# Right operands of the first feed-forward product, formed product by product, with their transposes between the early products

## The chip, the cores and the metric

One Trainium2 chip, one of its cores. The metric is the time of one execution on the device in microseconds, as the median of three runs. The engines are TensorE (PE, with its weight loads PEld), VectorE (DVE), ScalarE (ACT), GpSimd (POOL) and SyncE (SP, which issues the DMAs).

## The reference

A decoder block in float32: sequence 1024, model width 1024, one layer. Two branches (an RWKV-7 mix and a sparse attention) are merged by gates and projected back; then comes the feed-forward part with a hidden width of 4096, and a last norm. What matters here is its last third:

```python
x = x + merged @ w_out[l]
h2 = rms_norm(x, g_ffn[l])
x = x + jnp.square(jax.nn.relu(h2 @ w_ffn_up[l])) @ w_ffn_down[l]
return rms_norm(x, g_final)
```

## The kernel before

**Number format.** Each float32 operand of a large product is split into a high half (a copy to fp32r by ACT) and a low half (source minus high half, by DVE or POOL); `part` does that. A product is then three matmuls per block of 128 channels: high by high, high by low, low by high (`mm3`, lines 242 to 244). `mm3y` issues the same three through `pe`, which also ties each matmul to the one `window[0]` places earlier in the written order (a tie for the planner that adds no wait on the chip); `tr` does so for a transpose.

**Order of work.** The kernel is written as a sequence. A planner puts each instruction in its engine's queue when, by its own simulated costs, its inputs and a free room are there; earlier written instructions have precedence. Rooms of a tag (`bufs`) go round: a new tile waits until an old one is given back. The ties of `pe` bound how far TensorE's order may leave the written one.

**Gates and output projection** (lines 1328 to 1430). For eight blocks d of channels the gates are loaded into `gp`, a room of the tag `g8` (6 rooms of 128 x 2048 floats; d = 0 has one of its own), then tanh, products and sums give `merged[d]` (lines 1176 to 1186). The first loads of `x1` are tied behind the load of d = 7. Then `merged @ w_out` runs, c = 0 to 3, and its results are added to x (line 1430).

**Norm.** `normed(half)` forms the normalised rows `xs` of 512 tokens in two `g8` rooms (lines 1353 to 1357). `norm_first`, inside the output projection, transposes the first half of the tokens, keeps it as `raw0[0..7]` in two `g8` rooms ("hr") and forms the right operands R2 and R4.

**First feed-forward product.** h2 @ w_up is computed by Strassen's scheme with seven products of half size. For each of 16 blocks f of 128 + 128 hidden columns there are products 2, 4, 1, 5, 7, 3, 6, each of 4 x 3 matmuls of 128x512 with a right operand R[p] (the activations, made once for all f) and a left operand (weights, made per f). With B11 = raw0[0..3], B21 = raw0[4..7] and the second half of the tokens as B12 (pa) and B22 (pb), R2 = B11, R4 = B21 - B11, R1 = B11 + B22, R5 = B22, R7 = B21 + B22, R3 = B12 - B22, R6 = B11 + B12. `plan` lists entries: products (2, 4) of f = 0, 1, 2 first (PRE = 3; the early products), then (1, 5), (7, 3), (6) of f = 0, 1, 2, then all four entries of f = 3 and so on. The left operands are built two entries ahead (`up_ops`, `up_operands`): a load into `st` (3 rooms), a sum on POOL into `k2` (3 rooms, line 1462), then `part` into `w` (3 rooms). `up_product` adds results from the up rooms (6 of 128x512 in PSUM) to C (a `g8` room); after product 6 five sums are formed on DVE, three of them in kc (a `g8` room), and both are stored.

**norm_second** (lines 1386 to 1411) is called when the early products have all been written (i == PRE). For each k of 0 to 3 it transposes two blocks of the second half (`channels`, two rooms `small`), forms c1, c7, c6 and b22 in `k2` rooms, three of them by VectorE's scalar_tensor_tensor (STT) and b22 by ACT and later an STT, and splits each result into R1, R5, R7, R3 and R6 of that k.

The second feed-forward product (line 1540 on) follows; it uses `g8` for x1 (4 tiles) and o (4 tiles).

```python
            c1, c7, c6 = k2("c"), k2("c"), k2("c")
            STT(c1, pb, gb, raw0[k], op0=OP.mult, op1=OP.add)
            part(R[1][k][:, 0], R[1][k][:, 1], c1, nc.gpsimd)
```

Of the kernel before, what the change touches and what calls it, by code (L numbers as in the profile page):

```python
# [9 lines left out]
F32 = mybir.dt.float32  # L10
# [13 lines left out]
P = 128  # L24
# [71 lines left out]
def hybrid_block(ctx: ExitStack, tc: tile.TileContext, a, out, dbg=None, stop=99):  # L96
# [16 lines left out]
    def small():  # L113
        return psm_[0].tile([P, 512], F32, name="sm")
# [84 lines left out]
    def pull(gen, n):  # L199
        for _ in range(n):  # L200
            if next(gen, "end") == "end":
                return
# [1112 lines left out]
    psa[0] = psf_stack.enter_context(tc.tile_pool(name="psf", bufs=3, space=PSUM))  # L1315

    def g8(name):
        return mp.tile([P, 4, 512], F32, name=name, tag="g8", bufs=6)

    def k2(name):  # L1320
        return mp.tile([P, 512], F32, name=name, tag="k2", bufs=3)

    def part(hi, lo, src, eng):
        nc.scalar.activation(hi, src, AF.Copy)  # L1324
        eng.tensor_tensor(lo, src, hi.bitcast(F32), op=OP.subtract)  # L1325
# [3 lines left out]
    for d in range(8):  # L1329
        if d == 0:  # L1330
            gg, pp = gates1[0]
        else:
            gp = g8("gp")
            gg, pp = gp[:, 0:2], gp[:, 2]
            ld = gate_load(gg, pp, d, 1)
        if d % 2 == 0:
            w = next(ws)
        ps = acc()[:, 0:512]
        for k in range(4):
            mm3(ps, [w[:, s_, k, (d % 2) * P:(d % 2 + 1) * P] for s_ in range(2)],  # L1340
                [yT1[k][:, s_, :] for s_ in range(2)], start=(k == 0), stop=(k == 3))
        gate_merge(merged[d], gg, pp, ps)
# [14 lines left out]
            nc.vector.tensor_scalar(xs[j], xt[j], r[:, j:j + 1], None, op0=OP.mult)  # L1357
        return xs

    def channels(xs, k):  # L1360
        ps = small()
        for j in range(4):
            nc.tensor.transpose(ps[:, j * P:(j + 1) * P], xs[j][:, k * P:(k + 1) * P], ident)
        return ps, pcol("gffn", k)


    R = {}
    raw0 = []

    def norm_first():  # L1370
        xs = normed(0)
        room = [g8("hr") for _ in range(2)]
        raw0.extend(room[k // 4][:, k % 4] for k in range(8))
        for p in (2, 4):
            R[p] = [hp[0].tile([P, 2, 512], F32R, name="h2", tag=f"hT0_{4 * (p == 4) + k}") for k in range(4)]
        for k in (0, 4, 1, 5, 2, 6, 3, 7):
            ps, g = channels(xs, k)
            nc.scalar.activation(raw0[k], ps, AF.Copy, scale=g)
            if k < 4:
                part(R[2][k][:, 0], R[2][k][:, 1], raw0[k], nc.vector)  # L1380
            else:
                c = k2("c")
                nc.gpsimd.tensor_tensor(c, raw0[k], raw0[k - 4], op=OP.subtract)
                part(R[4][k - 4][:, 0], R[4][k - 4][:, 1], c, nc.vector)

    def norm_second(xs):
        def h2(k, n):
            if n < 8:
                return mp.tile([P, 2, 512], F32R, name="h2", tag="mh", bufs=8)
            if n < 18:  # L1390
                return mp.tile([P, 2, 512], F32R, name="h2", tag="x4", bufs=10)
            return base.tile([P, 2, 512], F32R, name="h2", tag="ev", bufs=2)

        for i, p in enumerate((1, 5, 7, 3, 6)):
            R[p] = [h2(k, 4 * i + k) for k in range(4)]
        for k in range(4):
            pa, ga = channels(xs, k)
            pb, gb = channels(xs, k + 4)
            STT = nc.vector.scalar_tensor_tensor
            c1, c7, c6 = k2("c"), k2("c"), k2("c")  # L1400
            STT(c1, pb, gb, raw0[k], op0=OP.mult, op1=OP.add)
            part(R[1][k][:, 0], R[1][k][:, 1], c1, nc.gpsimd)
            b22 = k2("c")
            nc.scalar.activation(b22, pb, AF.Copy, scale=gb)
            part(R[5][k][:, 0], R[5][k][:, 1], b22, nc.gpsimd)
            STT(c7, pb, gb, raw0[k + 4], op0=OP.mult, op1=OP.add)
            part(R[7][k][:, 0], R[7][k][:, 1], c7, nc.vector)
            STT(b22, pa, ga, b22, op0=OP.mult, op1=OP.subtract)
            part(R[3][k][:, 0], R[3][k][:, 1], b22, nc.vector)
            STT(c6, pa, ga, raw0[k], op0=OP.mult, op1=OP.add)  # L1410
            part(R[6][k][:, 0], R[6][k][:, 1], c6, nc.gpsimd)

    for c in range(4):
        if c == N2:
# [60 lines left out]
    def up_product(f, p, l):  # L1475
        ps = psu.tile([P, 512], F32, name="up")
        for k in range(4):
            mm3(ps, [l[s_][:, k] for s_ in range(2)], [R[p][k][:, s_] for s_ in range(2)],
                start=(k == 0), stop=(k == 3))
        if p == 2:  # L1480
            CB[f] = g8("C")
        c11, c12, c21, c22 = [CB[f][:, i] for i in range(4)]
        TT = nc.vector.tensor_tensor
        if p == 2:
            nc.scalar.activation(c22, ps, AF.Copy)
        elif p == 4:
            TT(c21, ps, c22, op=OP.add)
            nc.scalar.activation(c11, ps, AF.Copy)
            hidden(c21)
        elif p == 1:  # L1490
            TT(c11, ps, c11, op=OP.add)
            TT(c22, ps, c22, op=OP.subtract)
        elif p == 5:
            TT(c11, c11, ps, op=OP.subtract)
            nc.scalar.activation(c12, ps, AF.Copy)
        elif p == 7:
            TT(c11, ps, c11, op=OP.add)
            hidden(c11)
        elif p == 3:
            TT(c12, ps, c12, op=OP.add)  # L1500
            TT(c22, ps, c22, op=OP.add)
            hidden(c12)
        else:
            TT(c22, ps, c22, op=OP.add)
            hidden(c22)
            kc = g8("kc")
            TT(kc[:, 2], c11, c21, op=OP.add)
            TT(kc[:, 0], c11, c22, op=OP.add)
            TT(kc[:, 1], c12, c22, op=OP.add)
            nc.sync.dma_start(hc_dram[f, 4:7].rearrange("s p t -> p s t"), kc[:, 0:3])  # L1510
            TT(c12, c12, c11, op=OP.subtract)
            TT(c21, c21, c22, op=OP.subtract)
            nc.sync.dma_start(hc_dram[f, 0:4].rearrange("s p t -> p s t"), CB.pop(f))
# [21 lines left out]
        return up_operands(up_blocks(f, prods), prods)  # L1535

    ops = [up_ops(0), up_ops(1)]
    for i, (f, prods) in enumerate(plan):
        if i == PRE:
            norm_second(xs1)  # L1540
        l = ops.pop(0)
        for p in prods:
            up_product(f, p, l[p])
        ops.append(up_ops(i + 2))


# [63 lines left out]
    def square(t, i):  # L1610
        cs = slice(i * 512, (i + 1) * 512)
        if t not in ssq:
            if t % 2 == 0:
                o2 = g8("o").rearrange("p a b -> p (a b)")
                rooms.extend([o2[:, 0:D], o2[:, D:2 * D]])
            ssq[t] = mp.tile([P, 4], F32, name="ss", tag=f"ssf{t}"), rooms[t]
        ss, o = ssq[t]
        nc.scalar.activation(o[:, cs], x1[t][:, cs], AF.Square, accum_out=ss[:, i:i + 1])
# [88 lines left out]
```

## Time and profile before

| what | value |
|---|---|
| median of three runs | 1836.25 us (1833.04, 1836.25, 1837.2) |
| the profiled execution: time, span | 1827.06 us, 1825.3 us |
| mean granted TensorE clock in it | 0.961 |
| TensorE busy in it | 1692.4 us, 93% of the span |
| VectorE, ScalarE, GpSimd busy | 1320.5, 896.9, 841.7 us (72, 49, 46%) |
| DMA, mean over the span | 132 GB/s |

The profile tells of one execution; times in it run from the span's start. "Busy" is the time in which an engine has an instruction in work, waiting for a port or for memory included. The granted clock is a share of full speed. Shapes such as 128x512 are partitions by elements. The first feed-forward product lies between 1167 and 1497 us, the second from there to the end.

### The profile page before, as it was taken

Reading aid. Unit: us, or ns where it says so; the run is one execution under the profiler, and the core shown is the slowest. Engines: PE = TensorE matmul, PEld = TensorE weight load, DVE = VectorE, ACT = ScalarE, POOL = GpSimd, SP = SyncE. Lnnn points to the kernel's source line nnn. Section 1 sums busy time; section 2 is a strip of 40 time slices with the busy share of each in tenths; the row PEclk is TensorE's granted clock in tenths of the full one; section 3 lists DMA queues with packets and bytes.
Section 4 is the critical chain, followed back from the end, with each engine's and each line's share of the span. In section 5 each row is a group of like instructions: output and inputs, shape, how many; then the busy total and the mean of one; then the engine's idle time right before and its main releaser. Section 6 shows DMA issues by size and latency. Waiting matters only on the chain.

```text
span 1825.3 us, 27191 instructions
## 1 busy us (share of the span) xinstructions
PE 1692.4 (93%) x9554; PEld 1419.5 (78%) x9554; DVE 1320.5 (72%) x2597; ACT 896.9 (49%) x1751; POOL 841.7 (46%) x765
## 2 busy tenths in 40 slices
PE   6999999949999999998999898879999999999996
PEld 6988887738878777777877798857888887888884
DVE  6689946996777453678676556679888885765887
ACT  5375565717777434354535334544444444444443
POOL 1523566414343343343425432367666655545554
PEclk9999999979999998999878999999999999999998
DMA  5230353212311454345345466315545358643543
GB/s 173 75 116 29 116 144 105 66 41 89 116 35 36 138 151 132 99 137 163 109 123 170 154 226 251 105 60 170 174 137 180 128 185 299 207 141 91 171 124 127
DMA packets 267247, 241.52 MB, mean 132 GB/s; under 512 B 64268, under 2 KB 205894, under 8 KB 267110
## 3 DMA queue, kind: packets, MB, share of 16 engines
q1 hardware_dynamic: 267110, 239.78, 41.9%
q8 instruction: 75, 1.23, 0.3%
q14 instruction: 62, 0.51, 0.1%
HBM read 164.24 MB, written 75.50 MB: 131 GB/s over the span
## 4 chain that ended last, share of the span: by engine, by line
PE 60%; DVE 21%; DMA 8%; ACT 4%; issue 4%; POOL 2%; SPq 1%; DVEq 0%; ACTq 0%; POOLq 0%
PE dn L189 14%; PE up L243 8%; PE up L244 8%; PE up L242 8%; PE sm L189 5%; DVE jk L577 3%; DVE w L1325 2%; PE sm L192 2%; PE acc L189 2%; PE dn L243 2%; PE dn L244 2%; PE ch L189 2%; PE dn L242 2%; DMA zt<-zd 1%; DVE Zt L998 1%
## 5 line engine op out<-in xcount | busy, mean ns | idle before, releaser
L189 PE MATMUL dn<-hT,w 128*128 128x512 f32 (+1 forms) x1488 | 377.7, 401 | 8.3 <-ACT last L673 7.6
L189 PEld LDWEIGHTS dn<-hT,w 128*128 128x128 f32 (+1 forms) x1488 | 272.9, 188 | 67.1 <-ACT last L673 10.1
L1325 DVE TENSOR_TENSOR w<-st,w 128x512 fp32r<-128x512 f32 x224 | 236.6, 1089 | 78.7 <-ACT w L1324 78.3
L210 POOL TENSOR_TENSOR w<-st,w 128x1024 fp32r<-128x1024 f32 (+2 forms) x75 | 179.3, 2391 | 162.9 <-ACT w L209 143.7
L1324 ACT ACTIVATE w<-st 128x512 fp32r<-128x512 f32 x224 | 132.5, 624 | 168.2 <-PE up L244 50.8
L242 PE MATMUL up<-h,w 128*128 128x512 f32 x448 | 177.5, 397 | 7.4 <-ACT h L1324 5.9
L243 PE MATMUL up<-h,w 128*128 128x512 f32 x448 | 176.3, 394 | 2.2 <-DVE h L1325 1.4
L244 PE MATMUL up<-h,w 128*128 128x512 f32 x448 | 175.6, 393 | 1.6 <-DVE w L1325 1.6
L1588 POOL TENSOR_TENSOR st<-wb,wb 128x512 f32<-128x512 f32 x80 | 119.5, 1498 | 91.2 <-DVE w L1325 59.4
L243 PE MATMUL up<-w 128*128 128x512 f32 x384 | 150.2, 393 | 5.1 <-DVE ss L1606 3.3
L244 PE MATMUL up<-w 128*128 128x512 f32 x384 | 149.6, 392 | 0.0
L1462 POOL TENSOR_TENSOR c<-st 128x512 f32<-128x512 f32 x80 | 124.0, 1560 | 42.9 <-DVE w L1325 20.1
L209 ACT ACTIVATE w<-st 128x1024 fp32r<-128x1024 f32 (+2 forms) x91 | 94.7, 1041 | 42.9 <-PE acc L244 15.0
L242 PE MATMUL up<-w 128*128 128x512 f32 x384 | 108.0, 392 | 0.2
L242 PEld LDWEIGHTS up<-h,w 128*128 128x128 f32 x448 | 84.6, 189 | 28.5 <-ACT h L1324 9.2
L1473 POOL TENSOR_TENSOR C<-C 128x512 f32<-128x512 f32 x64 | 75.8, 1185 | 66.7 <-ACT C L1472 66.7
L577 DVE TENSOR_SCALAR_CACHE_REDUCE jk<-room,cand 128x384 bf16<-128x384 int16 (+2 forms) x96 | 92.7, 1009 | 15.1 <-ACT jk L590 14.1
L243 PEld LDWEIGHTS up<-h,w 128*128 128x128 f32 x448 | 85.0, 190 | 21.1 <-DVE h L1325 2.5
L244 PEld LDWEIGHTS up<-h,w 128*128 128x128 f32 x448 | 84.8, 189 | 21.2 <-DVE w L1325 3.3
L243 PE MATMUL dn<-w,hT 128*128 128x256 f32 (+1 forms) x320 | 91.6, 287 | 6.3 <-DVE w L210 6.3
L780 POOL TENSOR_SCALAR sm<-sm,rs 128x128 f32<-128x128 f32 (+7 forms) x64 | 47.8, 748 | 105.0 <-DVE rs L779 53.6
L590 ACT ACTIVATE jk<-room,neg 128x512 bf16<-128x512 int16 (+2 forms) x96 | 78.4, 819 | 33.2 <-POOL neg L598 21.6
(326 smaller groups left out, 4074.7 us busy)
## 6 DMA issues: line engine op xcount, KB each, us to landing
st<-hcd SPq DMA_DIRECT2D x112, 256.0 KB
st<-in_w_in SPq DMA_DIRECT2D x54, 512.0 KB
st<-in_w_ffn_up SPq DMA_DIRECT2D x35, 512.0 KB
hcd<-C SPq DMA_DIRECT2D x16, 1024.0 KB
wb<-in_w_ffn_down SPq DMA_DIRECT2D x64, 256.0 KB
hcd<-kc SPq DMA_DIRECT2D x16, 768.0 KB
zd<-ev SPq DMA_DIRECT2D x20, 512.0 KB
gzd<-ev SPq DMA_DIRECT2D x32, 256.0 KB
```

What stands on the lines that cost most here:

```text
L189: pe(nc.tensor.matmul(*args, **kw))
L209: nc.scalar.activation(hi, st[0:rows, 0:n], AF.Copy)
L210: (eng or nc.gpsimd).tensor_tensor(lo, st[0:rows, 0:n], hi.bitcast(F32), op=OP.subtract)
L242: nc.tensor.matmul(ps, l[0], r[0], start=start, stop=False, skip_group_check=shared)
L243: nc.tensor.matmul(ps, l[0], r[1], start=False, stop=False, skip_group_check=shared)
L244: nc.tensor.matmul(ps, l[1], r[0], start=False, stop=stop, skip_group_check=shared)
L577: nc.vector.tensor_scalar(junk, src[b], cand[:, j:j + 1], None, op0=OP.is_ge, op1=OP.add, accum_out=cnt[:, j:j + 1])
L590: nc.scalar.activation(junk, src[b], AF.Sign, bias=neg[:, j:j + 1], accum_out=cnt[:, j:j + 1])
L1324: nc.scalar.activation(hi, src, AF.Copy)
L1325: eng.tensor_tensor(lo, src, hi.bitcast(F32), op=OP.subtract)
L1462: nc.gpsimd.tensor_tensor(c, src, blocks[LEFT[p][2]], op=OP.add if LEFT[p][1] == "+" else OP.subtract)
L1588: nc.gpsimd.tensor_tensor(c, src, wblocks[RIGHT[p][2], f], op=OP.add if RIGHT[p][1] == "+" else OP.subtract)
```

## The change

The right operands R1, R5, R7, R3 and R6 are made by a generator, `norm_second`, which is pulled twice after each early product of f = 1 and f = 2, so its eight steps lie between them. The first four steps transpose B22 (k = 4 to 7) and form c1, b22 and, in place in `raw0`, B21 + B22, and split R1. The other four transpose B12, split R5 and form, in place, B11 + B12 in `raw0` and B12 - B22 in b22; the last of them then writes the splits of R7, R3 and R6, product by product. c1 lies in two rooms of the tag `ev`, b22 in two of `x4`; `k2` is left to the left operands. Blocks 2 and 3 of each four are transposed into up rooms, the others into `small`. The low halves are shared out by a list, eight on VectorE and twelve on GpSimd. The matmuls of the product and these transposes go through `mm3y` and `tr`, with a window of 8 until the entries up to (7, 3) of f = 0 are written, then 32. The tag `g8` has 4 rooms and a new tag `g8b` 2: gp of d = 1 and 4, hr, kc and o use `g8b`.

```diff
     def g8(name):
-        return mp.tile([P, 4, 512], F32, name=name, tag="g8", bufs=6)
+        return mp.tile([P, 4, 512], F32, name=name, tag="g8", bufs=4)
+
+    def g8b(name):
+        return mp.tile([P, 4, 512], F32, name=name, tag="g8b", bufs=2)
...
-            gp = g8("gp")
+            gp = g8b("gp") if d in (1, 4) else g8("gp")
...
-    def channels(xs, k):
-        ps = small()
+    def channels(xs, k, up=False):
+        ps = psu.tile([P, 512], F32, name="up") if up else small()
         for j in range(4):
-            nc.tensor.transpose(ps[:, j * P:(j + 1) * P], xs[j][:, k * P:(k + 1) * P], ident)
+            (tr if second else nc.tensor.transpose)(ps[:, j * P:(j + 1) * P], xs[j][:, k * P:(k + 1) * P], ident)
...
-        room = [g8("hr") for _ in range(2)]
+        room = [g8b("hr") for _ in range(2)]
...
+    ON_VECTOR = [(1, 1), (1, 3), (5, 1), (5, 3), (7, 1), (7, 3), (3, 1), (6, 1)]
...
-        for i, p in enumerate((1, 5, 7, 3, 6)):
-            R[p] = [h2(k, 4 * i + k) for k in range(4)]
+        c1, b22 = [], []
+        for _ in range(2):
+            t_ = base.tile([P, 2, 512], F32, name="c1", tag="ev", bufs=2)
+            c1 += [t_[:, 0], t_[:, 1]]
+            t_ = mp.tile([P, 2, 512], F32, name="b22", tag="x4", bufs=10)
+            b22 += [t_[:, 0], t_[:, 1]]
+        N_OF = {1: 0, 5: 4, 7: 8, 3: 12, 6: 16}
+        for p in (1, 5):
+            R[p] = [h2(k, N_OF[p] + k) for k in range(4)]
+        STT = nc.vector.scalar_tensor_tensor
+
+        def split(p, k, src):
+            part(R[p][k][:, 0], R[p][k][:, 1], src, nc.vector if (p, k) in ON_VECTOR else nc.gpsimd)
+
         for k in range(4):
-            pa, ga = channels(xs, k)
-            pb, gb = channels(xs, k + 4)
-            STT = nc.vector.scalar_tensor_tensor
-            c1, c7, c6 = k2("c"), k2("c"), k2("c")
-            STT(c1, pb, gb, raw0[k], op0=OP.mult, op1=OP.add)
-            part(R[1][k][:, 0], R[1][k][:, 1], c1, nc.gpsimd)
-            b22 = k2("c")
-            nc.scalar.activation(b22, pb, AF.Copy, scale=gb)
-            part(R[5][k][:, 0], R[5][k][:, 1], b22, nc.gpsimd)
-            STT(c7, pb, gb, raw0[k + 4], op0=OP.mult, op1=OP.add)
-            part(R[7][k][:, 0], R[7][k][:, 1], c7, nc.vector)
-            STT(b22, pa, ga, b22, op0=OP.mult, op1=OP.subtract)
-            part(R[3][k][:, 0], R[3][k][:, 1], b22, nc.vector)
-            STT(c6, pa, ga, raw0[k], op0=OP.mult, op1=OP.add)
-            part(R[6][k][:, 0], R[6][k][:, 1], c6, nc.gpsimd)
+            pb, gb = channels(xs, k + 4, k > 1)
+            STT(c1[k], pb, gb, raw0[k], op0=OP.mult, op1=OP.add)
+            nc.scalar.activation(b22[k], pb, AF.Copy, scale=gb)
+            STT(raw0[k + 4], pb, gb, raw0[k + 4], op0=OP.mult, op1=OP.add)
+            split(1, k, c1[k])
+            yield
+        for k in range(4):
+            pa, ga = channels(xs, k, k > 1)
+            split(5, k, b22[k])
+            STT(raw0[k], pa, ga, raw0[k], op0=OP.mult, op1=OP.add)
+            STT(b22[k], pa, ga, b22[k], op0=OP.mult, op1=OP.subtract)
+            if k == 3:
+                for p, src in ((7, raw0[4:8]), (3, b22), (6, raw0[0:4])):
+                    R[p] = [h2(k_, N_OF[p] + k_) for k_ in range(4)]
+                    for k_ in range(4):
+                        split(p, k_, src[k_])
+            yield
...
-            mm3(ps, [l[s_][:, k] for s_ in range(2)], [R[p][k][:, s_] for s_ in range(2)],
-                start=(k == 0), stop=(k == 3))
+            mm3y(ps, [l[s_][:, k] for s_ in range(2)], [R[p][k][:, s_] for s_ in range(2)],
+                 start=(k == 0), stop=(k == 3))
...
-            kc = g8("kc")
+            kc = g8b("kc")
...
     ops = [up_ops(0), up_ops(1)]
+    second = norm_second(xs1)
+    window[0] = 8
     for i, (f, prods) in enumerate(plan):
-        if i == PRE:
-            norm_second(xs1)
         l = ops.pop(0)
         for p in prods:
             up_product(f, p, l[p])
+            if 0 < i < PRE:
+                pull(second, 2)
+        if i == PRE + 1:
+            window[0] = PE_WINDOW
         ops.append(up_ops(i + 2))
...
-                o2 = g8("o").rearrange("p a b -> p (a b)")
+                o2 = g8b("o").rearrange("p a b -> p (a b)")
```

## Rows read from the trace of the kernel before

**Rows 1.** Stretches: bounds, length, busy time (instructions) by engine, clock, DMA share, GB/s.

```profile
1167.30:1183.72 16.42, 16.39 (x72) 13.57 (x73) 10.54 (x23) 7.93 (x15) 4.45 (x4) 1.00 0.28 97
1175.08:1218.80 43.72, 33.33 (x131) 22.98 (x130) 28.01 (x39) 22.91 (x40) 21.56 (x18) 0.92 0.09 25
1218.80:1260.00 41.20, 40.13 (x173) 32.23 (x174) 38.95 (x45) 14.93 (x27) 32.70 (x23) 1.00 0.48 160
1260.00:1496.65 236.65, 236.65 (x1042) 195.12 (x1040) 202.29 (x253) 102.05 (x177) 150.22 (x111) 1.00 0.46 159
```

**Rows 2.** Stretches, TensorE's matmuls into the up rooms alone.

```profile
1183.72:1218.80 35.08, 21.91 (x61) 0.90 0.11 30
```

**Rows 3.** TensorE in order of time: start, us, line, output<-inputs, count [idle before].

```profile
1147.58 0.60 PE L1363 MATMUL sm<-cst,xn 128*128 128x128 f32 x4
1147.94 0.36 PE L242 MATMUL acc<-w,mg 128*128 128x256 f32 x1
...
1167.33 0.47 PE L242 MATMUL up<-h,w 128*128 128x512 f32 x1 [0.94 <-DVE x L1430]
...
1183.50 0.39 PE L244 MATMUL up<-h,w 128*128 128x512 f32 x1
1183.74 1.03 PE L1363 MATMUL sm<-cst,xn 128*128 128x128 f32 x8
...
1218.86 0.50 PE L242 MATMUL up<-h,w 128*128 128x512 f32 x1 [0.48 <-ACT w L1324]
```

**Rows 4.** TensorE's waits, 1183.72 to 1496.6: us in total, times, longest.

```profile
PE up L242 <- ACT h L1324: 5.9, 7, 1.5
```

**Rows 5.** VectorE's waits, 1175.08 to 1218.8, the two longest.

```profile
DVE c L1401 <- PE sm L1363: 4.9, 2, 4.3
DVE c L1406 <- ACT c L1404: 4.7, 4, 1.3
```

**Rows 6.** VectorE in order of time.

```profile
1172.34 2.74 DVE L1357 TENSOR_SCALAR xn<-x,rq 128x1024 f32<-128x1024 f32 x4
...
1195.60 1.02 DVE L1325 TENSOR_TENSOR h<-c,h 128x512 fp32r<-128x512 f32 x1 [0.70 <-ACT h L1324]
...
1211.81 0.74 DVE L1410 SCALAR_TENSOR_TENSOR c<-sm,par,hr 128x512 f32<-128x512 f32 x1
```

**Rows 7.** Groups by line, VectorE then GpSimd, 1175.08 to 1218.8: busy us, mean ns.

```profile
L1325 DVE TENSOR_TENSOR h<-c,h 128x512 fp32r<-128x512 f32 x8 | 7.0, 877 | 2.2 <-ACT h L1324 2.1
L1325 DVE TENSOR_TENSOR w<-c,w 128x512 fp32r<-128x512 f32 x4 | 3.7, 956 | 0.0
L1325 DVE TENSOR_TENSOR w<-st,w 128x512 fp32r<-128x512 f32 x1 | 0.7, 684 | 0.0
...
L1325 POOL TENSOR_TENSOR h<-c,h 128x512 fp32r<-128x512 f32 x12 | 15.2, 1280 | 14.8 <-ACT h L1324 14.8
L1462 POOL TENSOR_TENSOR c<-st 128x512 f32<-128x512 f32 x3 | 3.8, 1286 | 2.3 <-DMA st<-in_w_ffn_up 1.6 <-DVE h L1325 0.7
L1473 POOL TENSOR_TENSOR C<-C 128x512 f32<-128x512 f32 x3 | 3.1, 1040 | 9.8 <-ACT C L1472 9.8
```

**Rows 8.** GpSimd in order of time.

```profile
1193.55 2.52 POOL L1325 TENSOR_TENSOR h<-c,h 128x512 fp32r<-128x512 f32 x2 [0.84 <-ACT h L1324]
```

**Rows 9.** SyncE, VectorE and ScalarE in order of time, at the gates.

```profile
1097.36 1.26 SPq L1176 DMA_DIRECT2D gp<-gzd  x1
...
1100.64 1.18 DVE L1186 SCALAR_TENSOR_TENSOR mg<-gp,mg 128x512 fp32r<-128x512 f32 x1
...
1110.85 1.04 ACT L1178 ACTIVATE gp<-gp 128x1024 f32<-128x1024 f32 x1
```

**Rows 10.** The chain that ended last, in order of time: start, us, what.

```profile
1083.70 6.42 DMA gp<-gzd
...
1211.37 1.29 POOL c L1462
1212.68 4.01 DMA st<-in_w_ffn_up
```

More of the change, by code (lines that the diff above doesn't have):

```diff
@@ L1358, in normed @@
         return xs
-    def channels(xs, k):
-        ps = small()
+    def channels(xs, k, up=False):
+        ps = psu.tile([P, 512], F32, name="up") if up else small()
         for j in range(4):
-            nc.tensor.transpose(ps[:, j * P:(j + 1) * P], xs[j][:, k * P:(k + 1) * P], ident)
+            (tr if second else nc.tensor.transpose)(ps[:, j * P:(j + 1) * P], xs[j][:, k * P:(k + 1) * P], ident)
         return ps, pcol("gffn", k)
     R = {}
-    raw0 = []
+    raw0, second = [], None
     def norm_first():
         xs = normed(0)
-        room = [g8("hr") for _ in range(2)]
+        room = [g8b("hr") for _ in range(2)]
         raw0.extend(room[k // 4][:, k % 4] for k in range(8))
```

## The prediction

> **What bounds the kernel now.** I looked first at the table of stretches over the first feed-forward product, because the diff touches little else. TensorE is busy for all of 1260 to 1496.65, and in the 16.4 us of the early products at full clock [rows 1]; between them, from 1183.72 to 1218.8, 61 of its product matmuls fill 21.9 of 35.1 us, at a granted clock of 0.90 [rows 2]. So one stretch has room in it, and it is the stretch of `norm_second`. Next I priced that room on TensorE itself. The 72 early matmuls start at 1167.33 and the last of them at 1183.50, 0.228 us from one to the next; four transposes take 0.36 us; the first of the second half's transposes comes at 1183.74, when all early products are over, and product (1,1), the first of block f = 1, starts at 1218.86 [rows 3]. If TensorE never waited, (1,1) would start at 1167.33 + 132 x 0.228 + 32 x 0.09 = 1200.3. So 18.6 us are lost there, and nothing can be won elsewhere: behind 1218.8 TensorE is short of 1.1 us in all [rows 1]. The waits name the cause: TensorE stands seven times, 5.9 us in all, before the high half of a right operand ("h") that ACT has not yet written [rows 4]; most of the rest are other such waits and matmuls that run slowly behind them.
>
> Then I asked what made the operands late. VectorE (DVE) is busy for only 28.0 of the 43.7 us from 1175.08, where the normalised rows are complete, to 1218.8; POOL for 21.6, ACT for 22.9 [rows 1]. DVE's idle time stands before the two kinds of step that start a round: 4.9 us for the transposes, 4.7 us for ACT's copy of B22 [rows 5]. None of these engines is full. It is a chain, four rounds one after the other: two transposed blocks in the two rooms of `small`, four results in the three rooms of `k2`, and the next round's transposes wait until both are free. The rows stand complete from 1172.34 + 2.74 = 1175.08 [rows 6], yet their transposes begin 8.7 us later.
>
> **Part by part.** *Transposes between the early products.* They stay 32, 2.9 us on TensorE. The pulls put the first eight behind (1,2), which ends at 1167.33 + 36 x 0.228 = 1175.5, and the rows are ready at 1175.08, so 0.4 us of cover; if that is gone TensorE waits for what is missing, and all of it is in the next term anyway. The last eight stand behind (2,4).
>
> *Rooms.* c1, b22 and the in-place sums in `raw0` take the place of `k2`, and four of the eight transposed blocks go to the up rooms. So STTs, splits and copies are limited by their engines and no longer by rooms. Their counts do not change: 16 STTs, 20 splits, of which 8 low halves on DVE and 12 on POOL, as before.
>
> *What is late next: DVE and POOL.* DVE must do, before (1,1) can start, the 28.0 us of the window [rows 1], the low half of (1,1)'s left operand, 0.96 by its kind [rows 7], and its 8 right low halves can grow from 0.88 [rows 7] to the 1.02 that one takes beside POOL [rows 6], 1.1 us. That is 30.1 us, and without a gap it ends at 1175.1 + 30.1 = 1205.2. But the engines do not run side by side in all of this. A DVE low half started at 1195.60 and took 1.02 us until 1196.62; POOL's two low halves ran from 1193.55 to 1196.07 [rows 6, 8], so DVE's ended 0.55 us after POOL's, and the same kind alone takes 0.68 [rows 7]. It waited. So I add them up as one queue: POOL 12 x 1.28 + 3 x 1.29 + 3 x 1.04 = 22.4 us, DVE 8 + 5 + 1 low halves at 0.55 to 0.68 = 7.7 to 9.5 us [rows 7], together 30.1 to 31.9. This queue opens with the low halves of (0,1) and (0,5) at about 1175.6 and stands empty some 1 us until the first right split (transposes, STT, ACT's high half), so it ends at 1206.7 to 1208.5. The page "SBUF — State Buffer" of the Trainium skill (section "SBUF: two separate sides") says that a VectorE instruction with two SBUF inputs and a GpSimd instruction hold a shared port pair by turns, each for its whole length. The row agrees. By that rule the end is the 1206.7 to 1208.5, without it 1205.2. It speaks against the change, which puts both kinds into less time.
>
> I take 1208.5 for the start of (1,1): the upper end, since two engines that feed each other will not pack without a hole. Bounds: 1205.2 without any, and 1212 with holes as large as the pieces of idle time before DVE that rooms do not make (the rest of 15.7 after 4.9 and 4.7 is 6.1 [rows 1, 5]; some 2.5 of it are in the 1208.5 already). So at (1,1) the gain is 10.4 us, between 6.9 and 13.7.
>
> *Behind (1,1).* In 1218.8 to 1260 DVE is busy for 38.95 of 41.2 us, so it is working off arrears already [rows 1]; more arrears could cost 0 to 2 us of TensorE. I take 0.4. From 1260 on DVE has 14% free and TensorE does not wait, so a gain is kept to the end, through a second feed-forward product that is TensorE's too.
>
> *Order ties.* `mm3y` and `tr` issue the same instructions as `mm3`; the ties only hold the planner to the written order within 8, later 32 instructions. In the dense stretch nothing waits [rows 1], so 0; in the early part it takes from TensorE the freedom to fill in, which is priced in the rivals.
>
> *g8 as 4 + 2 rooms.* C2 takes a room of the normalised rows and waits for the last transposes, as before; two of six up rooms hold (2,2) and (2,4) for some 3 us, and the products behind find others. hr, kc and o turn over in two rooms; kc comes once in 7 x 12 x 0.228 = 19 us, so 0. The gate loads are the one place with a price: d = 7 now waits for the room of d = 2 (low half at 1100.64, about 1.2 us) and not for that of d = 1 (its load went out at 1097.36), so SP issues it some 4.5 us later, and the four loads of x tied behind it too. Its tanh runs on ACT at 1110.85 only [rows 9], 13.5 us after the issue, while d = 1's load needed 6.4 us to land [rows 10]. The cover is then some 7 us, and I cost it at nothing. If the queue is fuller than that it costs up to 4.5 us. A gain is not excluded (other rooms come free in another order), 1 us at the most.
>
> **The sum.** 10.4 - 0.4 = 10.0 us. The profiled execution has a span of 1825.3 us and a time of 1827.06, 1.8 us around it; it would become 1815.3 and 1817.1. It lies 9.2 us below the median of the three timed runs, 1836.25. I take the difference off the median: 1826.25.
>
> **The rivals.** *TensorE alone sets the pace* (the planner packs all engines, arrears go to the dense stretch): (1,1) at 1200.3, gain 18.6, 1817.7. For it: idle time of 15.7 us on DVE. Against it: 30 us of queue do not fit into the 25 us from 1175.1 to 1200.3.
>
> *Product 6's sum is queued behind the splits.* The chain of waits that ended last runs through this place: POOL's sum for product 6's left operand starts at 1211.37, then the load that waited for its staging room lands 4.0 us later, and (1,1) follows 7.5 us after the sum's start [rows 3, 10]. Its `k2` room now comes free near 1176, so the planner can put it early into POOL's gaps. If it puts it behind the last right split instead, that split ends near 1207 and (1,1) starts near 1214.9: gain 4, 1832.3.
>
> *Slower: blocks stay serial and splits come after.* The splits of R7, R3 and R6 are now written behind the last block's STTs, 8 on POOL and 4 on DVE, 8 x 1.28 + 4 x 0.68 = 13.0 us by turns [rows 7]. Before, TensorE ran pieces of all five products between the rounds; now the order is held. If the in-place STT on b22 (which must wait for both halves of R5's split, one on POOL) blocks DVE's queue in each round, and with it evictions and low halves that stand behind, the last STT ends where it does now, 1211.81 + 0.74 [rows 6], less the 1.3 us by which the transposes of that part come earlier: 1211.2. Then (0,6) can end only near 1211.2 + 13.0 + 1 = 1225.2, 6.4 us behind the 1218.86 of now: 1842.6. It decides from a last STT later than 1204.8 on; my sum puts it near 1196 (1175.1 + 12 us of STTs, plus 9 us of other DVE work ahead of it). Against it: c1, b22 and raw0 are made early for all four blocks, so R1, R5 and R7 hang on nothing else.
>
> *Little happens:* the gate loads cost their 4.5 us and the packing is at its worse bound, gain 6.9 - 4.9 = 2: 1834.2.
>
> **How the numbers follow.** Forecast 0.58; TensorE alone 0.07; sum behind the splits 0.15; slower 0.10; little 0.10. About 0.2%, 3.7 us, is what a measurement of this kernel can tell from no change. Faster by more: 0.58 + 0.07 + two thirds of 0.15 + a fifth of 0.10 = 0.77. Within: 0.05 + 0.08 = 0.13. Slower: 0.10. The range from 1819 to 1836 has the forecast's bounds (gains of 5 to 13.7, with 1 us for the gate), the sum behind the splits and the little case; out of it lie the slower case, most of TensorE alone, and the edge of the little case, together under 0.2.
>
> **What would show it.** Right: transposes of 4 x 0.36 us behind (1,2), (1,4), (2,2) and (2,4); no wait of TensorE before 1186; (1,1) near 1208 (with the start of the stage at 1167); DVE busy over 90% from 1176 to (1,1), its low halves beside POOL above 1.0 us; what is left of the waits on R7 or R6, by DVE or POOL and no longer by rooms. Wrong: DVE idle by more than 5 us there (rooms or order still set it), the load for f = 1 issued later than (0,6) starts, the last STT behind 1204.8, a start of the stage later than 1169 (the gate), or waits of TensorE between 1260 and its end (the ties or the rooms).

## The result, and the profile after

The changed kernel takes 1820.11 us (median of 8 runs, 1815.13 to 1826.1) against 1830.77 us for the kernel before, timed beside it (median of 8, 1824.2 to 1838.85). The ratio is 0.9941, with a 95% interval from 0.9918 to 0.9965: 10.7 us faster, where 10.0 were forecast. The absolute forecast, 1826.25, is 6 us too high, nearly all of it from the base: the three runs that it started from had a median of 1836.25, 5.5 us above that of the eight.

The page of the changed kernel opens with its span and the busy time of the engines:

```profile
span 1818.7 us, 27190 instructions
PE 1696.2 (93%) x9554; PEld 1424.5 (78%) x9554; DVE 1326.4 (73%) x2597; ACT 894.9 (49%) x1751; POOL 846.9 (47%) x765
```

The profiled execution took 1820.43 us. Its span is only 6.6 us below the 1825.3 of before, because it reached the gates' product (the matmuls at the head of "Gates and output projection") late: at 1089.1 us, before at 1082.8. In the runs below, whose code up to there is that of before or of after, this point lies anywhere from 1076.8 to 1090.9. One row over 600 to 800 us, of before and then of after (columns as in [rows 1]), shows the same stretch at a lower granted clock:

```profile
600.00:800.00 200.00, 188.95 (x1119) 153.00 (x1117) 102.53 (x297) 75.55 (x157) 70.23 (x70) 0.91 0.44 120
```

```profile
600.00:800.00 200.00, 191.86 (x1089) 154.60 (x1088) 102.25 (x294) 72.70 (x152) 71.32 (x70) 0.87 0.43 117
```

So single spans don't tell these kernels apart, and I go by the stage: from the first to the last matmul of the first feed-forward product. It went from 329.1 to 317.5 us, 11.6 less. The way from the start of the gates' product to the stage went from 84.5 to 83.9, what lies behind the stage from 328.9 to 328.2.

The stretches of the stage, with all engines, answer [rows 1]:

```profile
1173.00:1193.00 20.00, 19.98 (x104) 16.72 (x105) 19.52 (x32) 14.69 (x28) 12.15 (x9) 1.00 0.35 121
1193.00:1208.65 15.65, 10.72 (x43) 7.10 (x41) 15.65 (x20) 8.91 (x16) 15.65 (x12) 1.00 0.12 35
1208.65:1265.00 56.35, 55.52 (x241) 44.79 (x242) 52.93 (x62) 21.75 (x40) 39.75 (x28) 1.00 0.46 154
1265.00:1490.50 225.50, 225.50 (x992) 186.03 (x991) 193.32 (x241) 96.64 (x169) 144.12 (x106) 1.00 0.46 158
```

TensorE now has room almost only in the 15.65 us from 1193, at full clock, and there VectorE and POOL (third and fifth busy number) are in work for every microsecond. TensorE in order of time, answering [rows 3]:

```profile
1181.29 0.38 PE L192 MATMUL sm<-cst,xn 128*128 128x128 f32 x2
...
1184.93 1.03 PE L192 MATMUL up<-cst,xn 128*128 128x128 f32 x8
...
1192.21 1.03 PE L192 MATMUL up<-cst,xn 128*128 128x128 f32 x8
...
1195.75 0.47 PE L189 MATMUL up<-h,w 128*128 128x512 f32 x1 [0.23 <-DVE hr L1419]
...
1204.72 0.98 PE L189 MATMUL up<-h,w 128*128 128x512 f32 x3 [1.84 <-DVE h L1328]
1207.10 0.97 PE L189 MATMUL up<-h,w 128*128 128x512 f32 x3 [1.41 <-POOL h L1328]
1208.65 24.53 PE L189 MATMUL up<-h,w 128*128 128x512 f32 x106 [0.58 <-DVE h L1328]
1234.01 26.22 PE L189 MATMUL up<-h,w 128*128 128x512 f32 x113 [0.83 <-DVE w L1328]
```

112 of the product's matmuls stand ahead of the row at 1208.65, so the 133rd, the first of (1,1) in written order, lies some 20 x 0.23 behind it, by its own record at 1213.4: 40.3 us after the start of the stage, before 51.5. It tells how far TensorE has come, no longer which product it is in, for the planner let (1,1) pass (0,6): VectorE makes R6's last low half and then adds the results of (1,1) (line 1512) and, much later, of (0,6) (line 1525) to C:

```profile
1213.81 1.13 DVE L1328 TENSOR_TENSOR h<-hr,h 128x512 fp32r<-128x512 f32 x1 [1.22 <-ACT h L1327]
1214.87 0.68 DVE L1512 TENSOR_TENSOR C<-up,C 128x512 f32<-128x512 f32 x1
...
1222.71 0.68 DVE L1525 TENSOR_TENSOR C<-up,C 128x512 f32<-128x512 f32 x1
```

(1,1) was done at 1214.87 at the latest, while (0,6) could not end before that half did, at 1214.94. The waits of TensorE in the stage, answering [rows 4] (us, times, longest):

```profile
PE up L189 <- DVE h L1328: 2.9, 3, 1.8
PE up L189 <- POOL h L1328: 1.8, 2, 1.4
PE up L189 <- DVE w L1328: 0.8, 1, 0.8
PE up L189 <- DVE hr L1419: 0.2, 1, 0.2
```

The seven waits for ACT's high halves are gone. What is left, 5.7 us (before 11.5), is nearly all for low halves by VectorE and POOL (line 1328); the largest are for R7 (1.84, at the 107th matmul) and R3 (1.41 and 0.58, at the 110th and 113th). The groups of low halves from 1181.61 to 1212.6, answering [rows 7] (busy us, mean ns):

```profile
L1328 POOL TENSOR_TENSOR h<-b,h 128x512 fp32r<-128x512 f32 x5 | 8.2, 1647 | 0.0
L1328 POOL TENSOR_TENSOR h<-hr,h 128x512 fp32r<-128x512 f32 x5 | 8.1, 1643 | 0.0
L1328 DVE TENSOR_TENSOR w<-c,w 128x512 fp32r<-128x512 f32 x6 | 7.1, 1203 | 0.0
L1328 DVE TENSOR_TENSOR h<-b,h 128x512 fp32r<-128x512 f32 x3 | 3.7, 1240 | 0.0
L1328 DVE TENSOR_TENSOR h<-hr,h 128x512 fp32r<-128x512 f32 x2 | 2.8, 1403 | 0.0
```

Both kinds became longer where they lie side by side: these of VectorE from 0.88 and 0.96 [rows 7] to 1.2 to 1.4 us, these of POOL from 1.28 to 1.65.

### The profile page after: what moved, and what is told of

Same layout as the page of the kernel before. It is cut to its first block, busy times and chain, and to the rows that moved or that the text cites. A ratio compares the mean times of both kernels' runs of the same rounds, so it can differ in the third digit from the quotient of the medians.

```text
span 1818.7 us, 27190 instructions
## 1 busy us (share of the span) xinstructions
PE 1696.2 (93%) x9554; PEld 1424.5 (78%) x9554; DVE 1326.4 (73%) x2597; ACT 894.9 (49%) x1751; POOL 846.9 (47%) x765
## 4 chain that ended last, share of the span: by engine, by line
PE 64%; DVE 22%; DMA 5%; ACT 3%; issue 3%; POOL 2%; SPq 1%; DVEq 0%; ACTq 0%; POOLq 0%
PE dn L189 16%; PE up L189 14%; PE sm L189 5%; PE up L243 4%; PE up L244 4%; PE up L242 3%; DVE jk L577 3%; PE ch L189 2%; DVE w L1328 2%; PE sm L192 2%; PE acc L189 2%; PE dn L243 2%; PE dn L244 2%; PE dn L242 2%; DMA zt<-zd 1%
## 5 line engine op out<-in xcount | busy, mean ns | idle before, releaser
L189 PEld LDWEIGHTS dn<-hT,w 128*128 128x128 f32 (+1 forms) x1488 | 275.1, 190 | 67.9 <-ACT last L673 10.1
L189 PE MATMUL up<-h,w 128*128 128x512 f32 x1344 | 310.5, 391 | 6.7 <-DVE h L1328 2.9
L243 PE MATMUL dn<-w,hT 128*128 128x256 f32 (+1 forms) x320 | 92.0, 289 | 6.3 <-DVE w L210 6.3
L242 PE MATMUL dn<-w,hT 128*128 128x256 f32 (+1 forms) x320 | 91.8, 289 | 0.8 <-ACT hT L272 0.8
L244 PE MATMUL dn<-w,hT 128*128 128x256 f32 (+1 forms) x320 | 91.8, 289 | 0.0
L243 PEld LDWEIGHTS up<-w 128*128 128x128 f32 x384 | 72.7, 189 | 22.1 <-DVE w L1328 6.5
L242 PEld LDWEIGHTS up<-w 128*128 128x128 f32 x384 | 72.6, 189 | 15.7 <-ACT w L1327 0.6
```

What stands on the lines that cost most here:

```text
L189: pe(nc.tensor.matmul(*args, **kw))
L242: nc.tensor.matmul(ps, l[0], r[0], start=start, stop=False, skip_group_check=shared)
L243: nc.tensor.matmul(ps, l[0], r[1], start=False, stop=False, skip_group_check=shared)
L244: nc.tensor.matmul(ps, l[1], r[0], start=False, stop=stop, skip_group_check=shared)
```

## The experiments

One number carries them: the stage. At 0.2277 us a matmul (16.17 us for 71 steps of the early ones [rows 3]) and 2.9 us of transposes it would last 1344 x 0.2277 + 2.9 = 308.9 if TensorE never waited. "Waits" is the sum of TensorE's waits inside it, "rest" what is left over 308.9. T1, against which the expectations are held, is the stage less 277.6 (before: 329.1 - 51.5), so it says nothing beyond the stage. "Count" is the start of the 133rd of the product's matmuls behind the stage's start. It differs from T1 by up to 2.0 us, since most kernels lose less behind that matmul than before did. In e10 and e12 the first of (1,1) is the 157th in written order; for them that is given, and T1 does not apply. "Clock" is the granted clock from 20 to 50 us behind the stage's start. Each row is one profiled execution; the stage of e7, which leaves it as it was, repeats that of before to 0.1 us, and no other stage was taken twice.

| kernel | stage | T1 | count | waits | rest | clock |
|---|---|---|---|---|---|---|
| before | 329.1 | 51.5 | 51.5 | 11.5 | 8.7 | 0.89 |
| after | 317.5 | 39.9 | 40.3 | 5.7 | 2.9 | 1.00 |
| e7_g8_split | 329.1 | 51.5 | 51.6 | 11.5 | 8.7 | 0.89 |
| e1_no_ties | 324.6 | 47.0 | 48.8 | 10.1 | 5.6 | 0.83 |
| e9_r3_first | 320.3 | 42.7 | 44.5 | 5.7 | 5.7 | 0.89 |
| e11_ties_alone | 330.8 | 53.2 | 52.8 | 14.3 | 7.6 | 0.66 |
| e2_late | 324.3 | 46.7 | 48.5 | 9.9 | 5.5 | 0.83 |
| e3_old_rooms | 331.9 | 54.3 | 54.7 | 15.4 | 7.6 | 0.77 |
| e4_low_on_act | 313.4 | 35.8 | 37.7 | 2.0 | 2.5 | 1.00 |
| e5_all_dve | 321.6 | 44.0 | 45.9 | 7.9 | 4.8 | 0.83 |
| e6_all_pool | 322.3 | 44.7 | 46.7 | 8.1 | 5.3 | 0.83 |
| e8_seven_early | 316.9 | 39.3 | 40.5 | 3.9 | 4.1 | 0.94 |
| e10_four_early | 317.0 | - | 43.4 | 5.3 | 2.8 | 1.00 |
| e12_squares_act | 311.6 | - | 41.2 | 1.1 | 1.6 | 1.00 |

### The room split alone: e7, on the kernel before

```diff
-        return mp.tile([P, 4, 512], F32, name=name, tag="g8", bufs=6)
+        return mp.tile([P, 4, 512], F32, name=name, tag="g8", bufs=4)
+
+    def g8b(name):
+        return mp.tile([P, 4, 512], F32, name=name, tag="g8b", bufs=2)
```

(gp of d = 1 and 4, hr, kc and o take `g8b`.)

> The kernel before with one part of the change alone: g8 as 4 rooms and g8b as 2, with gp of d = 1 and 4, hr, kc and o in g8b. Theory (the later load for d = 7 is covered): from the first matmul of the gates' product to the first of the feed-forward product 84 to 85 us, as in both kernels (84.5 and 83.9), and 51.5 us from there to (1,1). Rival (the load that goes out later costs up to 4.5 us): 87 to 89 us in the first distance.

The stage is that of before, with the same seven waits of 5.9 us, and the way from the gates' product to it is 84.8 us (84.5). The split does nothing by itself, and the later load of the gates is covered.

### Without the order ties: e1

```diff
-            (tr if second else nc.tensor.transpose)(ps[:, j * P:(j + 1) * P], xs[j][:, k * P:(k + 1) * P], ident)
+            nc.tensor.transpose(ps[:, j * P:(j + 1) * P], xs[j][:, k * P:(k + 1) * P], ident)
...
-            mm3y(ps, [l[s_][:, k] for s_ in range(2)], [R[p][k][:, s_] for s_ in range(2)],
+            mm3(ps, [l[s_][:, k] for s_ in range(2)], [R[p][k][:, s_] for s_ in range(2)],
```

> The changed kernel without the order ties: the matmuls of the first feed-forward product and the transposes of the second half of the tokens are issued as plain mm3 and transpose. Measured is the distance from the first matmul of the product to the first of product (1,1): 51.5 us in the kernel before, 39.7 in the changed one, 33.0 if TensorE never waited. Theory (rooms of their own and early transposes make the gain, the ties only hold the order): 39 to 42 us. Rival (the order held by the ties makes the gain, since the planner would otherwise put the transposes last): 46 us or more.

T1 is 47.0, in the rival's range: without the ties, which I had costed at nothing, the stage is 7.1 us longer. First TensorE of e1 in order of time, then VectorE:

```profile
1199.95 0.50 PE L242 MATMUL up<-h,w 128*128 128x512 f32 x1 [1.49 <-ACT h L1327]
...
1205.50 0.80 PE L243 MATMUL up<-h,w 128*128 128x512 f32 x1 [4.08 <-DVE h L1328]
1206.09 0.63 PE L244 MATMUL up<-h,w 128*128 128x512 f32 x1
1206.52 0.63 PE L242 MATMUL up<-h,w 128*128 128x512 f32 x1
```

```profile
1201.61 2.17 DVE L1328 TENSOR_TENSOR w<-c,w 128x512 fp32r<-128x512 f32 x2
1203.70 1.74 DVE L1328 TENSOR_TENSOR h<-b,h 128x512 fp32r<-128x512 f32 x1
```

TensorE stands 4.08 us for the low half of R3 (h<-b) that VectorE starts at 1203.70, 39.8 us after the start of the stage, behind two low halves of left operands (w) that nobody needs yet. In after the corresponding one starts at 1207.10, 34.1 behind the start. Then the matmuls come every 0.43 us: the 15 from 1205.50 to 1211.62 take 6.1 us, 2.7 more than at 0.228. With 4.4 us more of waits (10.1 against 5.7) that makes the 7.1. The 4.4 come from the order, as the next run shows; the 2.7 lie in matmuls at a lower clock, whose fall no run ties to the order (last section).

### R3's low half ahead of the left operands: e9, on e1

```diff
-            part(w[:, 0, cs], w[:, 1, cs], src, nc.vector)
+            ins = part(w[:, 0, cs], w[:, 1, cs], src, nc.vector)
+            if first:
+                after(r3[0], ins)
```

(`first` holds for the entry (1, 5) of f = 1; `r3[0]` is the low half of R3, k = 1; the tie binds the planner's order only.)

> The changed kernel without the order ties (e1), with one tie on VectorE in their place: the low halves of the left operands of (1,1) and (1,5) stand behind R3's low half for block 1 in VectorE's queue. Without ties (1,1) came at 47.0 us (length of the stage less 277.6), with 4.1 us of wait in one piece for that half, and a fallen clock behind it. Theory (what the ties bring is the planner's order on VectorE, where that half stood behind left operands that nobody needs yet): 42 to 45 us, and the wait of 4.1 us under 2.5. Rival (TensorE's own order, which the ties hold, is what matters): 46 to 48 us.

T1 is 42.7, as its theory said, and TensorE's waits come down from 10.1 to 5.7, those of after. VectorE in order of time:

```profile
1206.75 0.72 DVE L1328 TENSOR_TENSOR h<-b,h 128x512 fp32r<-128x512 f32 x1
1207.39 3.21 DVE L1328 TENSOR_TENSOR w<-c,w 128x512 fp32r<-128x512 f32 x2
```

One low half put ahead of two on VectorE gives 4.3 of the 7.1 us. The 2.8 that are left stand in the rest, 5.7 against 2.9: the 12 matmuls from 1205.09 to 1211.51 take 5.7 us without their wait of 0.68, 3.0 more than at 0.228. So in this place the ties of TensorE's matmuls act through another engine's queue. That the rest too is theirs is not shown: e8 below has the ties, and its clock falls as well.

### Ties without the rest: e11, on the kernel before

`mm3y` in `up_product`, `tr` for the second half's transposes, a window of 8 and later 32.

> The kernel before with the order ties alone (windows of 8 and 32 on the matmuls of the first feed-forward product and on the transposes of the second half of the tokens); norm_second, its rooms and its place stay as before. (1,1) came at 51.5 us in the kernel before (length of the stage less 277.6). Theory (ties bring something only where the operands come product by product; with rounds block by block they take from TensorE the filling in): 52 to 57 us. Rival (the ties alone bring the 7 us that their loss cost): 43 to 47.

T1 is 53.2, as its theory said. The ties alone make before 1.7 us slower: TensorE waits 12.8 us before transposes for rooms (before 1.2), where before ran matmuls that are now held behind. The ties pay only once the rooms are there.

### The place and the rooms: e2 and e3

e2 forms the same operands in the same rooms, but behind the early products:

```diff
+        if i == PRE:
+            pull(second, 8)
...
-            if 0 < i < PRE:
-                pull(second, 2)
```

> The changed kernel with its eight steps pulled in one go when the early products have all been written, as the kernel before calls them; rooms, in-place sums, product order, shares and ties stay. Distance from the first matmul of the product to (1,1): 51.5 us before, 39.7 changed. Theory (both parts count: VectorE and GpSimd have some 30 us to do by turns, and here most of it can begin only 16.4 us after the start in place of 8.2): 43 to 46 us. Rival 1 (the rooms make all of it): 39 to 41. Rival 2 (the early start makes all of it): 50 or more.

T1 is 46.7, so with the new rooms the early place is worth 6.8 us. That is just above its theory (by count, 48.5, between the theory and rival 2). Its largest waits are

```profile
PE up L189 <- DVE h L1328: 6.4, 4, 4.0
PE sm L192 <- DVE hr L1419: 2.9, 1, 2.9
```

e3 keeps the early place and the ties, but works block by block in the three rooms of `k2`, as before (the old body of `norm_second`, one k a pull).

> The opposite half: the old body of norm_second (four rounds, c1, c7, c6 and b22 in the three rooms of k2, transposed blocks in small, splits block by block), one round behind each early product of f = 1 and 2, with the ties and the 4 + 2 rooms of g8. Distance from the first matmul of the product to (1,1): 51.5 us before, 39.7 changed. Theory (rounds of 6.65 us stay a chain, from 8.2 us on; the products of f = 0 follow in order after the last round, and the sum for product 6 waits for its k2 room): 43 to 47 us. Rival 1 (the early transposes make all of it): 39 to 41. Rival 2 (the rooms make all of it): 50 or more.

T1 is 54.3, worse than before and 7 us above its theory. The wait shows the chain of rooms:

```profile
PE sm L192 <- DVE c L1413: 9.0, 3, 5.9
```

By number that is rival 2, the rooms alone, but e2 shows that they do not make it either. Against before, early transposes with old rooms lose 2.8 us, new rooms late gain 4.8, both together 11.6, all three with the ties. The fair base for them is e11, which has the ties too and lacks only the room split that e7 found worth nothing: 330.8 with neither, 331.9 with the early place, 324.3 with the rooms, 317.5 with both. So the early place costs 1.1 us with the old rooms and gives 6.8 with the new; the rooms give 6.5 late and 14.4 early. "Rooms" stands here for the whole new body of `norm_second`: its rooms, the splits product by product, the up rooms for four blocks and the new shares of the low halves. No run takes these apart.

### Who forms the low halves: e4, e5, e6

e4 puts the twelve low halves of POOL on ACT as plain copies, which leaves out their subtraction; it prices the load and is no kernel to use:

```diff
+            if (p, k) in ON_VECTOR:
+                part(R[p][k][:, 0], R[p][k][:, 1], src, nc.vector)
+            else:
+                nc.scalar.activation(R[p][k][:, 0], src, AF.Copy)
+                nc.scalar.activation(R[p][k][:, 1], src, AF.Copy)
```

> The changed kernel with the twelve low halves that GpSimd makes of R1, R5, R7, R3 and R6 replaced by ScalarE copies of the source (so the subtraction of the high half is left out in them). It takes 12 x 1.28 us off GpSimd and leaves VectorE's instructions as they are. Distance from the first matmul of the product to (1,1): 39.7 us changed, 33.0 without any wait. Theory (VectorE and GpSimd take turns, and their sum sets the rest of 6.7 us): 34 to 36.5 us, and VectorE's low halves fall towards 0.7 us each. Rival (VectorE's own work sets it): 38.5 to 40.

T1 is 35.8, as its theory said; by count 37.7, between the theory and the rival, so 2.7 of the 4.1 us lie ahead of the 133rd matmul and the others behind it. Two of the groups of VectorE, in the 31 us that answer those shown of after:

```profile
L1328 DVE TENSOR_TENSOR w<-c,w 128x512 fp32r<-128x512 f32 x7 | 4.6, 679 | 0.0
...
L1328 DVE TENSOR_TENSOR h<-b,h 128x512 fp32r<-128x512 f32 x3 | 2.0, 677 | 0.0
```

In after they take 1203 and 1240 ns (h<-hr, beside POOL's sums, still takes 1062, after 1403). So POOL's twelve low halves beside VectorE's are worth 4.1 us of the stage, at a clock of 1.00 in both. e5 (`ON_VECTOR` holds all twenty) and e6 (`ON_VECTOR = []`) shift it to one side.

> The changed kernel with all twenty low halves of the right operands on VectorE (eight before). Distance from the first matmul of the product to (1,1): 39.7 us changed. Theory (turns: a low half holds GpSimd's turn for 1.28 us but VectorE's for 0.6, so twelve moved save 8 us of turns, while VectorE's own work without waits grows from 23 to 30 us): 39 to 42. Rival (VectorE's busy time sets it and waits are part of its work: 30 + 12 x 0.88 us): 47 or more.

> The changed kernel with all twenty low halves of the right operands on GpSimd (twelve before). Distance from the first matmul of the product to (1,1): 39.7 us changed. Theory (turns: eight moved add 8 x (1.28 - 0.6) = 5.4 us to the common queue): 43 to 47. Rival (VectorE's own work sets it, and loses 8 us of it): 34 to 38.

e6 came as its theory said, 44.7 (count 46.7). e5, 44.0 (45.9), lies between its theory and the rival: the count of turns forecast it some 2 to 4 us too early. TensorE and then VectorE of e5:

```profile
1206.33 15.93 PE L189 MATMUL up<-h,w 128*128 128x512 f32 x58 [6.09 <-DVE h L1328]
```

```profile
1205.12 2.96 DVE L1328 TENSOR_TENSOR h<-b,h 128x512 fp32r<-128x512 f32 x4
```

Nearly all of its waits is one: R3's low halves stand late in VectorE's queue, as in e1. The four take 0.74 us each on average, so it is not their length. Whether all on VectorE is worse in itself, or only in this order, is not told apart.

### R7 split as early as R5: e8

`split(7, k, raw0[4 + k])` stands right behind `split(5, k, b22[k])`.

> The changed kernel with the splits of R7 written into the loop over k, directly behind those of R5, ahead of the sums for R6 and R3. Distance from the first matmul of the product to (1,1): 39.7 us changed. Theory (the sum of VectorE's and GpSimd's turns sets the end, and the order within it moves little): 38.5 to 40.5. Rival (the place of R7's splits behind the last block's sums makes the waits): 36 to 38.

T1 is 39.3: as its theory said, within 0.6 us of after. Its waits are 1.8 us shorter, its clock in the stretch a little lower (0.94), and the one nearly eats the other.

### A fourth early product pair: e10, and the squares on ACT: e12

```diff
-    PRE = 3
+    PRE = 4
```

> The changed kernel with PRE = 4 in place of 3: products 2 and 4 of a fourth block come early, so the first right operand of the late kind is needed 5.4 us later (one more load of 512 KB is issued). Theory (VectorE and GpSimd need about 31 us from the complete rows on, whatever TensorE does, so 5.4 us more of early products cover most of the 7 us still lost): the stage shortens by 3 to 6 us against the changed kernel, to 312 to 314.5 us from 317.5; time ratio to the kernel before 0.990 to 0.993. Rival (VectorE and GpSimd only push their arrears behind, into a stretch where they are nearly full): 316.5 to 318, ratio 0.993 to 0.996.

The stage is 317.0: the rival was right, half a microsecond is won. The waits only move, to the left operands' low halves:

```profile
PE up L189 <- DVE w L1328: 3.1, 3, 1.9
```

Timed, it takes 1820.44 us against 1827.57 of before, ratio 0.9953 [0.9931, 0.9975], no different from after. In its profile 3.7 us more than in after lie behind the stage (331.9 us; the same in e6), of which 1.5 are a longer wait for left operands where the second product starts (6.0 against 4.5); the others no run explains.

e12 takes in addition the squares from POOL:

```diff
-        nc.gpsimd.tensor_tensor(h, h, h, op=OP.mult)
+        nc.scalar.activation(h, h, AF.Square)
```

> The kernel with four early blocks (e10) and the 64 squares of the hidden blocks formed by ScalarE from the result of its own relu, where GpSimd formed them (64 x 1.18 us off GpSimd, about 64 x 0.6 more on ScalarE, which is busy for less than half of the stage). The stage took 317.5 us in the changed kernel, 317.0 with four early blocks, 329.1 before. Theory (VectorE and GpSimd take turns, and arrears from the early stretch only moved on, since both are nearly full behind it): 311 to 314 us, no wait of TensorE over 1 us in the stage, ratio to the kernel before 0.989 to 0.993. Rival (VectorE's own work sets the end, or ScalarE's longer queue takes GpSimd's place): 316 to 318 us, ratio 0.994 to 0.997.

The stage is 311.6, as its theory said and 2.7 us above the 308.9, and the time 1812.55 us (median of 6) against 1831.11 of before: ratio 0.9908 [0.9885, 0.9931], the lowest of the three that were timed; its interval still overlaps that of after. Its stretches:

```profile
1189.70:1219.70 30.00, 28.89 (x125) 22.59 (x123) 29.74 (x36) 20.49 (x39) 25.25 (x17) 1.00 0.24 69
1219.70:1481.30 261.60, 261.60 (x1150) 215.66 (x1150) 202.92 (x285) 143.73 (x248) 107.86 (x68) 1.00 0.48 165
```

TensorE is full from 1219.70 on, with 1150 matmuls in 261.60 us. In the whole kernel POOL is busy for 769.8 us (after 846.9), VectorE for 1293.9 (1326.4), and VectorE's instructions are the same 2597, so what it saves must be waiting. The squares were not moved with three early pairs, so the shares of the two edits are not known.

## Why the prediction was right, and which term was mis-sized

*The place and the cause: right.* Of the stage's 11.6 us, 11.2 are won ahead of the 133rd matmul, and rooms were the reason that the early place could not pay before: with the old ones it loses (e3), with the new ones VectorE is busy for 97% of the time from 1176 to the 133rd matmul.

*VectorE and POOL as one queue: right in this order.* Forecast was (1,1) 41.2 us after the start of the stage; the 133rd matmul came at 40.3. VectorE's low halves beside POOL took 1.2 to 1.4 us ("above 1.0"), POOL's grew too, and with POOL's low halves on ACT two groups of VectorE's fell to 0.68 and the stage by 4.1 us (e4). The rule that I cited from the Trainium skill (page "SBUF — State Buffer", section "SBUF: two separate sides"), of a port pair held by turns, agrees with these numbers. The hole that I added for two engines which feed each other hardly shows: both are busy for the whole of the 15.65 us before 1208.65, and 40.3 lies between the two ends of the queue without a hole (39.4 and 41.2). The same count of turns failed for e5, so it holds only where the order within the queues is that of need.

*Behind (1,1): small, but of the other sign.* I took 0.4 us more as lost there; from the 133rd matmul on the stage took 277.6 us before and 277.2 in after, with one wait of 0.83 us at 1234.01.

*The transposes: in place.* The first lie at 1181.29, 8.3 us after the start: directly behind the 36th matmul, the end of (1,2), and between the first three of (1,4). The rows were complete only at 1181.69, so the cover of 0.4 us was gone, but no wait came of it. The others follow behind 48, 60 to 64 and 72 matmuls, as forecast; the last end at 1193.2. No wait of TensorE comes before 1195.75, 22.7 us after the start (forecast: none in 18.7). The last STT starts at 1206.44, 33.4 us after the start, where the sum had some 29 and the sign of being wrong was 37.5. What is left of the waits is on R7, which was forecast, and on R3, where R6 was.

*The gates: right.* The load for d = 7 goes out 19.5 us after the start of the gates' product, before 14.5: 4.9 us later, where I said 4.5. SyncE and ACT in after:

```profile
1108.56 0.37 SPq L1176 DMA_DIRECT2D gp<-gzd  x1
```

```profile
1117.55 1.04 ACT L1178 ACTIVATE gp<-gp 128x1024 f32<-128x1024 f32 x1
```

The tanh stands 28.5 us after that start, before 28.0 [rows 9], so the load is hidden. The stage starts at 1173.0, behind the 1169 that I had named as a sign of being wrong, but by 6.3 us that this execution had lost before the gates' product.

*The order ties: the term that was mis-sized.* "In the dense stretch nothing waits, so 0" was true of the dense stretch; for the early part, the prediction named only what the ties take from TensorE. There 7.1 of the 11.6 us go without them, 4.4 of them waits and 2.7 at a lower clock. The step overlooked that a tie on TensorE changes what the planner puts first on VectorE: without it, low halves for later products go ahead of the one that TensorE stands for. The sum came out because it had assumed that VectorE works in the order of need; the ties are what makes it so, and that is luck. Had they been left out, the stage would have gained 4.5 us, and the working as written would still have forecast 10.

*The clock: a term that the sum does not have.* Of the 11.6 us, 5.8 are fewer waits and 5.8 are rest, with the granted clock at 1.00 in place of 0.89. The forecast took TensorE at full pace without a reason why its clock would hold. It held in after; in e8, with nearly the same waits, it fell, and the rest was 1.2 us longer. So a part of the agreement, of about this size, may be luck too.

*The rivals.* TensorE alone (1200.3, 33.0 after the start) is not reached: the two low-half engines lie between. Product 6's sum is in none of TensorE's waits. The slower case, a late last STT with the splits behind it, did not come; e3 is a serial chain too, but through its old rooms.

*Open.* Why TensorE's clock fell in e8 and e9 and not in after; e5 between its theories; what the parts of the new body are worth; most of the 3.7 us behind the stage in e10 and e6; the shares of the two edits in e12.

## What to carry to other kernels

Give a serial chain rooms before giving it an earlier place: here, with the ties everywhere, the earlier place cost 1.1 us with the old rooms and gave 6.8 with the new. Where a planner orders the queues, a tie on one engine is to be costed on the others: look at what stands just ahead of the instruction that the bounding engine waits for, and ask whether it is needed sooner. And when VectorE and POOL are both full with two-input work, count their operations as one queue for a first estimate, and look for a third engine, here ACT, for part of it.

## What the runs showed of the hardware

TensorE's clock cost as much as a middling wait, and in e1 it fell ahead of the longest wait, not in it. Three kernels in pieces of 2 us (matmul busy time and count, granted clock); first e1, then e8, then after:

```profile
1198.00:1200.00 2.00, 0.51 (x3) 1.00 0.00 0
1200.00:1202.00 2.00, 1.39 (x3) 0.71 0.00 0
1202.00:1204.00 2.00, 0.00 (x0) 0.50 0.00 0
```

```profile
1200.00:1202.00 2.00, 0.98 (x3) 1.00 0.00 0
1202.00:1204.00 2.00, 0.72 (x2) 0.83 0.00 0
1204.00:1206.00 2.00, 2.00 (x6) 0.50 0.00 0
```

```profile
1202.00:1204.00 2.00, 0.87 (x4) 1.00 0.00 0
1204.00:1206.00 2.00, 0.98 (x3) 1.00 0.00 0
1206.00:1208.00 2.00, 0.90 (x3) 1.00 0.00 0
```

In e1 the clock had gone to the lower of its two levels (1.2 GHz, 0.50) before the wait of 4.08 us began, behind waits of 1.71 and 1.49; in e9 it fell behind 1.71 and 1.31 (0.66 from 1204 to 1206, then 0.50). But e8 and after have nearly the same waits in the same places: 0.29, 0.40, 1.79 and 1.40 in e8, the last two 31.1 and 33.5 us after the stage's start; 0.23, 0.47, 0.41, 1.84 and 1.41 in after, the last two at 31.7 and 34.1. After stayed at 1.00, and e8 fell to 0.50. So in these runs the waits alone do not settle whether the clock falls; what does is open. The price is in the table: where the clock stayed at 1.00 the rest is 1.6 to 2.9 us, where it fell 4.1 to 8.7. So a forecast of this stage that knows its waits to a microsecond is still open by 1 to 3 us (e8 and e9 against after).
